# One evacuation step for two heads, with DMAs that bring the halves to the heads' tiles

## The chip, the cores and the metric

The kernel runs on one core of a Trainium2 chip. A core has a matrix engine (TensorE, PE in the profile, with its weight loads shown apart as PEld), three engines for elementwise work (VectorE, DVE; ScalarE, ACT; GpSimd, POOL) and a queue engine (SyncE, SP) that issues most of the DMAs here. Every engine works through its own instructions in order; semaphores make one wait for another. Matrix products land in PSUM, and ACT or DVE must bring them from there to SBUF ("evacuate" them) before TensorE can use them as operands or the PSUM tile can be filled again.

The metric is the device time of one execution in microseconds (us). Before the change it is 707.76 us, the median of three runs (707.51 to 709.02).

## The reference

One layer on a sequence of 1024 tokens of width 1024. The input is normalised and modulated to `u`; one projection `h = u @ w_in` gives queries, keys, values, gates and forget logits for 8 + 8 heads of width 64. Eight heads are forgetting attention, eight stick-breaking attention, both causal; the gated outputs go through `w_out`, a residual and a last layer norm.

```
h = u @ w_in
fq, fk, fv, fg, ff, sq, sk, sv, sg = _split_columns(h)
# forgetting heads
s = einsum('bhqd,bhkd->bhqk', q, k) * scale + (f_q[..., :, None] - f_k[..., None, :])
p = softmax(where(causal, s, -inf));  y = p @ v
# stick-breaking heads
z = einsum('bhqd,bhkd->bhqk', q, k) * scale
later = cumsum(log_keep, axis=3, reverse=True) - log_keep
w = where(strict, exp(log_sigmoid(z) + later), 0);  y = w @ v
y = concat([y_fox * silu(fg), y_sb * silu(sg)]) @ w_out
x = layer_norm(alpha * x + gate * y, ln_g, ln_b)
```

## The kernel before

**Precision.** All large products take fp32 values as a rounded part ("hi") and a rest ("lo"), and add three products: hi by hi, lo by hi, hi by lo. So each evacuation of queries and keys makes two pieces: a rounded copy on ACT and the rest (product minus the rounded copy) on DVE.

**Pairs.** The 16 heads are handled as eight pairs `p` = 0 to 7; 0 to 3 are stick-breaking, 4 to 7 forgetting. A pair's two heads `h` stand in the two halves of the 128 partitions of a projection: head 0 in partitions 0 to 63, head 1 in 64 to 127. Pairs 0 and 1 are projected in a start phase; the later ones by `gen_m(p, m)` with `m` = 0 for queries, 1 for keys and 2 for gates. `gen_m` fetches two weight halves (`fetch_m`), and then makes two chunks `ch` of 512 tokens, each 24 matmuls (L256 to L258) into one of two PSUM tiles `acc`, and evacuates each chunk at its end.

**The tiles of the heads.** For each head, `qst[p][h]` holds the rounded queries in the head's own 64 partitions and the rest in the other 64. `kst[p][h]` holds the rounded keys twice, once in each half. One matmul over all 128 partitions (L410) then gives hi by hi plus lo by hi. The third product (L411) takes the keys' rest, `klo[p]`, which holds both heads, against a query tile that is zero in the other head's partitions.

**The evacuation of queries and keys.** `evac_q` (L227) makes, for each head, one ACT step (L232) and one DVE step (L233) on 64 partitions. DVE writes its result into the other half of partitions. `evac_k` (L236) makes, for each head, one ACT step (L241), one DMA that copies the rounded keys to the other half (L243), and one DVE step (L244).

**The ring.** Split weights lie in a ring `whi`/`wlo` of five slots (`RING = 5`, `ring_w`). A weight half is fetched raw by SP into one of two raw tiles (L121), and split by POOL into a ring slot (L125, L126). A slot is free when the last matmul that reads it has run. Value weights, the output weights (which go back to DRAM, L770 and L771) and the attention outputs that are read back at the end (L788 to L792) use the same ring.

**Attention.** A unit is a pair, a head and a block of 128 queries; there are 128 units. A unit has scores (L410, L411), a softmax or stick-breaking part on ACT, DVE and POOL, a transpose on PE (L456) two units later, and the product with the values (L471).

**What sets the order.** The order of TensorE's instructions is written out by hand: the loop at L927 emits a unit's scores, and between them steps of the list `fillers` (projections, values) as the table `FILL` says. The last projection of keys, `gen_m(7, 1)`, ends just before the units of pair 7 begin. Pair 7 starts with the last block, which needs keys of all 1024 tokens. The orders of ACT, DVE, POOL and SP come from a planner at build time: it plays the program on a timeline of its own and gives each engine the earliest-written instruction that is ready there. On the chip each queue keeps that order, whatever is ready first. Around pair 7 SP also loads attention outputs (`yr`, L788), the residual input (`xr`, L823) and the output weights (`woh`, `wol`, L761 and L762). ACT's queue loads a forget row (`fb`, L375).

Of the kernel before, what the change touches and what calls it, by code (L numbers as in the profile page):

```python
# [8 lines left out]
F32 = mybir.dt.float32  # L9
F32R = mybir.dt.float32r  # L10
AF = mybir.ActivationFunctionType
ALU = mybir.AluOpType

P = 128
# [4 lines left out]
HD = 64  # L19
EPS = 1e-5  # L20
ALPHA = 2.0 ** 0.25
SCALE = HD ** -0.5
# [5 lines left out]
def tile_hybrid_layer(  # L28
# [17 lines left out]
    nc = tc.nc  # L46
# [15 lines left out]
    def acc_tile(name):  # L62
        return ps.tile([P, 512], F32, tag="acc", bufs=2, name=name)
# [52 lines left out]
    def ring_w(key):  # L116
        return [sb.tile([P, 528], F32R, tag=tag, bufs=RING, name=f"{tag}_{key}") for tag in ("whi", "wlo")]
# [14 lines left out]
    def fetch_m(p, m):  # L132
        return [fetch_half(p, m, h) for h in range(2)]
# [93 lines left out]
    def evac_q(p, ch, acc, qst, heads):  # L227
        s = slice(ch * 512, ch * 512 + 512)
        for h in heads:
            r = slice(h * HD, h * HD + HD)  # L230
            o = slice((1 - h) * HD, (1 - h) * HD + HD)
            nc.scalar.activation(qst[h][r, s], acc[r, :], AF.Copy, scale=SCALE)  # L232
            nc.vector.scalar_tensor_tensor(qst[h][o, s], acc[r, :], SCALE, qst[h].bitcast(F32)[r, s],  # L233
                                           op0=ALU.mult, op1=ALU.subtract)

    def evac_k(p, ch, acc, kst, klo, heads):  # L236
        s = slice(ch * 512, ch * 512 + 512)
        for h in heads:
            r = slice(h * HD, h * HD + HD)
            o = slice((1 - h) * HD, (1 - h) * HD + HD)  # L240
            first = nc.scalar.copy(kst[h][r, s], acc[r, :])  # L241
            kf = kst[h].bitcast(F32)
            nc.sync.dma_start(kf[o, s], kf[r, s])  # L243
            last = nc.vector.tensor_tensor(klo[r, s], acc[r, :], kf[r, s], op=ALU.subtract)  # L244
        return first, last

    def evac_g(p, ch, acc, sg):
        s = slice(ch * 512, ch * 512 + 512)
        nc.scalar.activation(sg[:, s], acc, AF.Tanh, scale=0.5)
        nc.vector.scalar_tensor_tensor(sg[:, s], sg[:, s], 1.0, acc, op0=ALU.add, op1=ALU.mult)  # L250

    def m_step(acc, tiles, kt, ch):
        hi, lo = tiles[kt // 4]
        c = slice((kt % 4) * P, (kt % 4) * P + P)
        s = slice(ch * 512, ch * 512 + 512)
        nc.tensor.matmul(acc, hi[:, c], u_hi[kt][:, s], start=(kt == 0), stop=False)  # L256
        nc.tensor.matmul(acc, hi[:, c], u_lo[kt][:, s], start=False, stop=False)  # L257
        nc.tensor.matmul(acc, lo[:, c], u_hi[kt][:, s], start=False, stop=(kt == NB - 1))  # L258

    qst, kst, klo, sgt, vt = {}, {}, {}, {}, {}  # L260
# [11 lines left out]
    def evac_m(p, m, ch, acc, heads=(0, 1)):  # L272
        if m == 0:
            evac_q(p, ch, acc, qst[p], heads)
        elif m == 1:
            return evac_k(p, ch, acc, kst[p], klo[p], heads)
        else:
            evac_g(p, ch, acc, sgt[p])

    def gen_m(p, m):  # L280
        tiles = fetch_m(p, m)
        yield
        (make_q, make_k, make_g)[m](p)
        for ch in ((1, 0) if m == 2 and p >= 4 else (0, 1)):
            acc = acc_tile(f"m_{p}_{m}_{ch}")
            for kt in range(NB):
                m_step(acc, tiles, kt, ch)
                if kt == NB - 1:
                    evac_m(p, m, ch, acc)
                if kt % 2 == 1:  # L290
                    yield

# [426 lines left out]
    for kb in range(NB):  # L719
# [5 lines left out]
        if kb < len(evacs):  # L725
            n, h = evacs[kb]
# [140 lines left out]
    def gen_last_g(p):  # L867
# [12 lines left out]

    fillers = chain([
        beside(chain([gen_v(0, v0_w, range(4, NB)), gen_m(1, 2)]), gen_gate()),
        gen_m(2, 0), gen_m(2, 1), gen_v(1),
        beside(chain([gen_m(2, 2), gen_m(3, 0), gen_m(3, 1), gen_m(3, 2)]), gen_forget()),
        gen_m(4, 0), gen_m(4, 1), gen_v(2),
        beside(chain([gen_m(4, 2), gen_m(5, 0), gen_m(5, 1), gen_m(5, 2),
# [40 lines left out]
    for k in range(len(units) + LAG + 1):  # L927
        if k < len(units):
# [10 lines left out]
            p, h, i = units[k]  # L939
# [85 lines left out]
```

## Time and profile before

| | |
|---|---|
| time, median of 3 runs | 707.76 us (707.51 to 709.02) |
| profiled execution, first to last instruction (span) | 705.8 us |
| PE busy | 680.8 us, 96% of the span |
| PE weight loads | 593.0 us, 84% |
| DVE busy | 509.6 us, 72% |
| POOL busy | 422.4 us, 60% |
| ACT busy | 378.8 us, 54% |
| DMA queue of SP | 32.4% of 16 engines' span |

Of the profiled execution the profile tells the span alone; the median of the runs is 1.96 us above it. Times in the profile are counted from the first instruction. A row of the timeline gives start, duration, engine, line, operation, what it writes and reads, shape, and in brackets the idle time of the engine before it and what ended that. A row of the groups gives count, busy time and the mean duration in ns, then the idle time before. A row of the waits gives who waited for whom, the total, the times and the longest. A busy PE is made of matmuls whose ends are modelled and which overlap, so its gaps are read from the waits.

### The profile page before, as it was taken

To read this page: it belongs to the slowest core of one execution; us is meant where nothing else is said; L and a number is where in the kernel's file an instruction comes from. 1 tells how busy PE (TensorE), PEld (TensorE's weight loads), DVE (VectorE), ACT (ScalarE), POOL (GpSimd) and SP (SyncE) were. 2 spreads that over 40 slices of the span, in tenths; PEclk is the share of its full clock that TensorE was granted. 3 is DMA by queue.
4 is the path that set the end of the run, shared out by engine and by line. 5 is a ranking of instruction groups with operands and counts; after the bars stand their busy time and mean duration, and the time that the engine had idled before them with its cause. 6 is when DMAs were issued, how large, how long until landed. Compare 5 with 4: busy or idle time off the path is not lost. (4 is left out here: it accounts for less than half of the span.)

```text
span 705.8 us, 11791 instructions
## 1 busy us (share of the span) xinstructions
PE 680.8 (96%) x4033; PEld 593.0 (84%) x4033; DVE 509.6 (72%) x963; ACT 378.8 (54%) x856; POOL 422.4 (60%) x523
## 2 busy tenths in 40 slices
PE   7999998989999999999999999999999999999995
PEld 4789887878998888889998887889988889888884
DVE  5985689897858697788686685757676767774644
ACT  4667346756658566666665563646564666621000
POOL 4560258665629675857388897868583455665412
PEclk9999999999999999999999999999999999999999
DMA  8953451101101212112034554435241189143301
GB/s 306 415 212 126 132 167 35 28 26 53 53 7 37 70 37 67 43 38 68 9 124 155 176 170 137 134 105 165 92 148 53 56 271 371 48 162 113 121 32 59
DMA packets 44027, 81.59 MB, mean 116 GB/s; under 512 B 5120, under 2 KB 18880, under 8 KB 43072
## 3 DMA queue, kind: packets, MB, share of 16 engines
q1 hardware_dynamic: 42816, 76.65, 32.4%
q10 hardware_dynamic: 1152, 4.19, 2.1%
q8 instruction: 32, 0.52, 0.3%
q14 instruction: 27, 0.22, 0.1%
HBM read 60.34 MB, written 16.29 MB: 109 GB/s over the span
## 5 line engine op out<-in xcount | busy, mean ns | idle before, releaser
L256 PE MATMUL m<-uh,whi 128*128 128x512 f32 x304 | 126.4, 416 | 0.0
L257 PE MATMUL m<-ul,whi 128*128 128x512 f32 x304 | 119.9, 394 | 0.0
L258 PE MATMUL m<-uh,wlo 128*128 128x512 f32 x304 | 119.7, 394 | 0.0
L459 DVE TENSOR_TENSOR pt<-T,pt 128x512 fp32r<-128x512 f32 (+2 forms) x192 | 100.5, 549 | 14.6 <-ACT pt L458 13.3
L439 POOL TENSOR_TENSOR be<-be,kp 128x127 f32<-128x127 f32 (+3 forms) x64 | 79.0, 1235 | 47.0 <-DVE kp L437 44.3
L458 ACT CAST pt<-T 128x512 fp32r<-128x512 f32 (+2 forms) x192 | 85.8, 480 | 18.6 <-PE T L456 14.8
L471 PEld LDWEIGHTS pv<-pt,v 128*128 128x128 f32 x640 | 83.9, 188 | 10.4 <-DVE pt L459 5.2
L471 PE MATMUL pv<-pt,v 128*128 128x256 f32 (+1 forms) x640 | 85.1, 277 | 4.5 <-DVE pt L459 3.6
L437 DVE TENSOR_TENSOR_SCAN kp<-kp 128x128 f32<-128x128 f32 (+6 forms) x56 | 82.6, 1476 | 1.9
L424 POOL TENSOR_SCALAR a<-a,l 128x1024 f32<-128x1024 f32 (+3 forms) x64 | 48.3, 755 | 41.7 <-DVE l L423 28.1
L422 ACT ACTIVATE a<-a,nm 128x1024 f32<-128x1024 f32 (+3 forms) x64 | 49.8, 779 | 40.8 <-DVE nm L417 38.9
L410 PE MATMUL S<-k,q 128*128 128x512 f32 (+5 forms) x192 | 66.8, 349 | 2.3 <-ACT be L430 1.7
L258 PEld LDWEIGHTS m<-uh,wlo 128*128 128x128 f32 x304 | 57.1, 188 | 13.6
L411 PE MATMUL S<-kl,qz 128*128 128x512 f32 (+5 forms) x192 | 65.5, 342 | 0.0
L256 PEld LDWEIGHTS m<-uh,whi 128*128 128x128 f32 x304 | 57.3, 189 | 8.8 <-DVE kl L244 0.4
L257 PEld LDWEIGHTS m<-ul,whi 128*128 128x128 f32 x304 | 57.4, 189 | 8.0
L480 POOL TENSOR_TENSOR ty<-ty,sg 64x256 f32<-64x256 f32 x64 | 48.8, 762 | 19.7 <-DVE ty L479 9.8
L434 DVE TENSOR_TENSOR_SCAN kp<-kp,ident 128x128 f32<-128x128 f32 x64 | 42.0, 656 | 24.4 <-ACT kp L429 21.1
L417 DVE CUSTOM_DVE_ANT_0 a<-S,fb 128x1024 f32<-128x1024 f32 (+3 forms) x64 | 48.2, 754 | 15.7 <-issue 6.5
L429 ACT ACTIVATE kp<-S 128x128 f32<-128x128 f32 (+3 forms) x64 | 41.7, 652 | 32.9 <-PE S L411 31.4
L126 POOL TENSOR_TENSOR wlo<-raw,whi 128x512 fp32r<-128x512 f32 x38 | 56.8, 1496 | 3.4 <-DMA wo_dr<-wlo_o 1.8
L311 PE MATMUL v<-whi_v,uh 128*128 128x256 f32 (+1 forms) x192 | 56.0, 292 | 1.1 <-DVE kl L244 1.1
(280 smaller groups left out, 1633.2 us busy)
## 6 DMA issues: line engine op xcount, KB each, us to landing
raw<-in_w_qkg_dram SPq DMA_DIRECT2D x38, 256.0 KB, 2.7
wss<-in_w_ss_dram SPq DMA_DIRECT2D x7, 1024.0 KB, 8.5
x<-in_x_dram SPq DMA_DIRECT2D x8, 512.0 KB, 7.6
k<-k SPq DMA_DIRECT2D x32, 128.0 KB, 2.2
wg<-in_w_gate_dram SPq DMA_DIRECT2D x8, 512.0 KB, 5.2
raw_o<-in_w_out_dram SPq DMA_DIRECT2D x16, 256.0 KB, 2.6
fb<-f_dr ACTq DMA_DIRECT2D x8, 512.0 KB, 4.2
wo_dr<-whi_o SPq DMA_DIRECT2D x16, 256.0 KB, 2.5
```

The costliest lines, as they stand in the source:

```text
L126: nc.gpsimd.tensor_tensor(lo[:, :n], raw, hi.bitcast(F32)[:, :n], op=ALU.subtract)
L256: nc.tensor.matmul(acc, hi[:, c], u_hi[kt][:, s], start=(kt == 0), stop=False)
L257: nc.tensor.matmul(acc, hi[:, c], u_lo[kt][:, s], start=False, stop=False)
L258: nc.tensor.matmul(acc, lo[:, c], u_hi[kt][:, s], start=False, stop=(kt == NB - 1))
L311: nc.tensor.matmul(acc[:, :n], u_hi[kt][:, ts_], hi[:, s], start=(kt == 0), stop=False)
L410: nc.tensor.matmul(S[:, s, :w], qst[p][h][:, qs], kst[p][h][:, ks], start=True, stop=False)
L411: nc.tensor.matmul(S[:, s, :w], z, klo[p][:, ks], start=False, stop=True)
L437: nc.vector.tensor_tensor_scan(rv, rv, rv, initial=kp[:, ke - P:ke - P + 1], op0=ALU.mult, op1=ALU.min)
L439: nc.gpsimd.tensor_tensor(be[:, :ke - 1], be[:, :ke - 1], kp[:, 1:ke], op=ALU.mult)
L458: nc.scalar.copy(hi[:, :n, qo:qo + P], t3)
L459: nc.vector.tensor_tensor(lo[:, :n, qo:qo + P], t3, hi.bitcast(F32)[:, :n, qo:qo + P], op=ALU.subtract)
L471: nc.tensor.matmul(acc[:, q0:256], vt[p][:, kb, h * P:(h + 1) * P], pt[:, kb % 4, q0:], start=(part == 0 and kb == 0), stop=(part == 1 and ...
```

## The change

For pairs 2 to 7 the chunks of queries and keys are evacuated by two new functions. Each makes one ACT step and one DVE step on all 128 partitions, that is on both heads at once. The pieces that belong to other partitions or to the other head's tile are brought there by DMAs on SP's queue.

For queries, the rounded part and the rest go to a pair of tiles from the ring `whi`/`wlo`, and four DMAs of 64 partitions carry them from there to `qst`. For keys, ACT writes both heads' rounded keys into `kst[p][0]`, and DVE makes `klo` in one step. Then two DMAs copy head 1's rows to both halves of `kst[p][1]`, and a third copies head 0's rows over head 1's rows in `kst[p][0]`. The start phase (pairs 0 and 1) keeps the old functions.

```diff
+    def evac_q_pair(p, ch, acc, qst):
+        s = slice(ch * 512, ch * 512 + 512)
+        hi, lo = (t[:, :512] for t in ring_w(f"q_{p}_{ch}"))
+        nc.scalar.activation(hi, acc, AF.Copy, scale=SCALE)
+        nc.vector.scalar_tensor_tensor(lo, acc, SCALE, hi.bitcast(F32), op0=ALU.mult, op1=ALU.subtract)
+        for part in range(2):
+            for h in range(2):
+                r = slice(h * HD, h * HD + HD)
+                to = slice((h ^ part) * HD, (h ^ part) * HD + HD)
+                nc.sync.dma_start(qst[h].bitcast(F32)[to, s], (hi, lo)[part].bitcast(F32)[r, :])
+
+    def evac_k_pair(p, ch, acc, kst, klo):
+        s = slice(ch * 512, ch * 512 + 512)
+        a, b = slice(0, HD), slice(HD, P)
+        nc.scalar.copy(kst[0][:, s], acc)
+        nc.vector.tensor_tensor(klo[:, s], acc, kst[0].bitcast(F32)[:, s], op=ALU.subtract)
+        k0, k1 = (t.bitcast(F32) for t in kst)
+        nc.sync.dma_start(k1[b, s], k0[b, s])
+        nc.sync.dma_start(k1[a, s], k0[b, s])
+        nc.sync.dma_start(k0[b, s], k0[a, s])
+
...
                 if kt == NB - 1:
-                    evac_m(p, m, ch, acc)
+                    if m == 0:
+                        evac_q_pair(p, ch, acc, qst[p])
+                    elif m == 1:
+                        evac_k_pair(p, ch, acc, kst[p], klo[p])
+                    else:
+                        evac_m(p, m, ch, acc)
```

## The prediction

> **What bounds the kernel now.** I read the page's sums first, then the busy time by stretches, then TensorE's waits in the stretch of the change.
>
> ```profile
> PE 680.8 (96%) x4033; PEld 593.0 (84%) x4033; DVE 509.6 (72%) x963; ACT 378.8 (54%) x856; POOL 422.4 (60%) x523
> ```
>
> ```profile
> 150.00:572.00 422.00, 417.38 (x2621) 373.13 (x2619) 307.90 (x597) 253.74 (x593) 285.30 (x335) 1.00 0.28 86
> 572.00:692.00 120.00, 119.77 (x611) 100.38 (x610) 77.55 (x164) 35.97 (x90) 58.40 (x75) 1.00 0.43 156
> ```
>
> The columns after the window's length are PE, PE weight loads, DVE, ACT, POOL, the granted clock, the DMA engines' busy share and GB/s. All changed evacuations lie between 150 and 572 us. There TensorE is busy 417.4 of 422 us at full clock, and after that, until its last matmuls, 119.8 of 120. Its order is fixed, so a stall there comes out at the end nearly whole, and a gain can't be larger than the waits it still has:
>
> ```profile
> PE pv L471 <- DVE pt L459: 2.1, 3, 1.5
> PE v L311 <- DVE kl L244: 1.1, 1, 1.1
> PE pv L471 <- ACT pt L458: 0.7, 1, 0.7
> PE S L410 <- DVE nm L417: 0.4, 1, 0.4
> ```
>
> These are all its waits from 150 to 572 us: 2.1 + 1.1 + 0.7 + 0.4 = 4.3 us. That is the most that the change can win. Only the second (1.1 us) is on an instruction that the change touches. So TensorE bounds this stage, not ScalarE (254 of 422 us) or VectorE (308).
>
> Here a rule speaks the other way. The Trainium skill, page "Perfetto Trace Analysis", section "Identifying the Most-Contended Engine", says that matmul busy time is a poor measure of TensorE's headroom and that the weight loads' share should be used. By it 422 − 373.1 = 48.9 us would be open here, and the 13.8 us of ScalarE time below could come off whole. The waits in the rows above contradict that: 4.3 us is what TensorE waited for others.
>
> **The change part by part.** *ACT and DVE steps.* By shape, the groups are:
>
> ```profile
> L233 DVE SCALAR_TENSOR_TENSOR q<-m,q 64x512 fp32r<-64x512 f32 x24 | 16.5, 688 | 6.6 <-ACT q L232 6.1
> L244 DVE TENSOR_TENSOR kl<-m,k 64x512 fp32r<-64x512 f32 x24 | 16.5, 686 | 4.8 <-ACT k L241 4.6
> L232 ACT ACTIVATE q<-m 64x512 fp32r<-64x512 f32 x24 | 14.2, 592 | 7.9 <-PE m L258 7.2 <-DVE q L233 0.2
> L241 ACT CAST k<-m 64x512 fp32r<-64x512 f32 x24 | 13.9, 581 | 10.9 <-PE m L258 8.8 <-DVE kl L244 1.9
> L250 DVE SCALAR_TENSOR_TENSOR sg<-sg,m 128x512 f32<-128x512 f32 x14 | 9.5, 679 | 2.2 <-ACT sg L249 2.2
> L249 ACT ACTIVATE sg<-m 128x512 f32<-128x512 f32 x14 | 8.4, 597 | 5.3 <-PE m L258 5.3
> ```
>
> The gate rows show that 128 partitions cost what 64 do (597 against 592 ns, 679 against 688 ns). So 48 ACT steps (14.2 + 13.9 = 28.1 us) become 24 of 597 ns (14.3 us): 13.8 us less. 48 DVE steps (33.0 us) become 24 of 679 ns (16.3 us): 16.7 us less. Neither engine sets the end, so this counts only through the waits above. The 1.1 us wait is this place:
>
> ```profile
> 184.74 0.69 DVE L244 TENSOR_TENSOR kl<-m,k 64x512 fp32r<-64x512 f32 x1
> 185.49 0.39 PE L311 MATMUL v<-whi_v,uh 128*128 128x264 f32 x1 [1.10 <-DVE kl L244]
> ```
>
> The second head's DVE step frees the PSUM tile late. With one step per chunk it goes: −1.1 us. What is late next there is nothing that the waits show. The other 3.2 us come from transposes and softmax, which the change doesn't touch; the engines' busy time falls by 5% (13.8 of 253.7 and 16.7 of 307.9), and as waits in a queue fall faster than the load I estimate −0.4 us (bounds 0 and −3.2). Relief: −1.5 us, bounds 0 and −4.3.
>
> *SP's queue.* Queries get 4 DMAs a chunk (48 in all), keys 3 where they had 2 (12 more): 60 more issues.
>
> ```profile
> L243 SPq DMA_DIRECT2D k<-k x32: 461/472/588, 49.8 to 569.3; - x32
> DMA to landing us min/median/max: 2.2/2.2/7.5
> ```
>
> 60 × 0.472 = 28.3 us of SP's time over 422 us, and 60 × 128 KB = 7.9 MB on DMA engines that are 28% busy. What they delay on SP's queue (raw weights, outputs of heads) has slack: no wait of TensorE above names a DMA. So 0. Without that cover it costs at most what a transfer lies behind, four issues or 1.9 us at each of 12 chunks. The queries themselves are needed many units later, and 2.2 us of landing lies beside projections.
>
> *The third copy of keys.* It overwrites rows that DVE and the first two copies read, so it waits on SP until these have landed, and everything behind it on SP waits too. Mostly nobody is near: the keys of pairs 2 to 6 are finished long before their scores. The last chunk of pair 7 is the exception:
>
> ```profile
> 565.85 0.58 ACT L241 CAST k<-m 64x512 fp32r<-64x512 f32 x1 [0.75 <-PE m L258]
> ```
>
> ```profile
> 566.46 0.47 SPq L243 DMA_DIRECT2D k<-k  x1
> 568.32 0.36 SPq L788 DMA_DIRECT2D yr<-y_dr  x1
> 568.77 0.44 SPq L823 DMA_DIRECT2D xr<-in_x_dram  x1
> 569.30 0.47 SPq L243 DMA_DIRECT2D k<-k  x1
> 569.82 0.61 SPq L762 DMA_DIRECT2D wol<-wo_dr  x1
> 570.48 0.54 SPq L761 DMA_DIRECT2D woh<-wo_dr  x1
> ```
>
> ```profile
> 571.76 0.40 PE L410 MATMUL S<-k,q 128*128 128x512 f32 x1
> ...
> 577.64 0.50 PE L410 MATMUL S<-k,q 128*128 128x512 f32 x1
> ```
>
> The matmul at 571.76 is the second half of pair 7's first scores (head 0). Before, its copy left at 566.46, with 5 us to spare. The matmul at 577.64 is head 1's; its copy left at 569.30. After, ACT ends at 566.4, the two head 1 copies leave at 566.5 and 566.9 (0.47 apart) and land 2.2 to 2.7 us later, at about 569.3. Only then can the third leave, and it now carries head 0's keys. That is the moment of the old copy at 569.30, whose landing, that of the one at 566.46, and that of `woh` (570.48) are:
>
> ```profile
> L243 SPq DMA_DIRECT2D k<-k x1: 467/467/467, 569.3 to 569.3; - x1
> DMA to landing us min/median/max: 7.5/7.5/7.5
> ...
> L243 SPq DMA_DIRECT2D k<-k x1: 467/467/467, 566.5 to 566.5; - x1
> DMA to landing us min/median/max: 2.7/2.7/2.7
> ...
> DMA to landing us min/median/max: 9.1/9.1/9.1
> ```
>
> Behind the two large loads (568.32 and 568.77) the copy took 7.5 us, to 576.8. So the matmul waits from 571.76 to 576.8: +5.0 us, and TensorE, in order, with it. The nearest bounds: 0, if it lands in the median 2.2 us (569.3 + 2.2 = 571.5); and +7.8, if it falls behind the output weights' first loads too and lands with `woh` (570.5 + 9.1 = 579.6). Below 0 nothing is possible, since the scores can't start earlier than TensorE's order has them. I take +5.0, the row at the same moment. Of it comes back what TensorE waits for others later, 0.2 us (the gap of 0.23 in 120 us, above): −0.2.
>
> On this place two rules of the Trainium skill's page "DMA: Bandwidth & Descriptors" pull apart. Its section "Anatomy of one DMA" gives a fixed 2.0 us plus bytes over 436 GB/s (fitted on another path), 2.3 us for 128 KB; the copy would then land in time and the sum be 5 us lower. Its section "Queues, rings and completion order" says that descriptors of a queue are consumed in ring order, which puts the copy behind the loads before it. The 7.5 us row agrees with the second.
>
> *The ring.* The 12 query chunks now also take a slot of the five. POOL fills every slot as soon as it is free:
>
> ```profile
> 157.87 0.63 POOL L125 TENSOR_SCALAR whi_v<-raw_v 128x528 fp32r<-128x528 f32 x1 [0.71 <-PE m L257]
> ...
> 396.61 0.40 PE L258 MATMUL m<-uh,wlo 128*128 128x512 f32 x1
> ...
> 401.10 0.40 PE L256 MATMUL m<-uh,whi 128*128 128x512 f32 x1
> ```
>
> The first row is a weight split that waited for a slot. So at the end of a query's first chunk there is often no free slot. Its evacuation then waits until the first weight half is freed, 12 matmuls later. From there to the first matmul of the next projection, which needs the same PSUM tile, I count 4.1 us in the tightest place (397.0 to 401.1, last two rows). The evacuation takes 0.60 + 0.68 us and its turn on two busy engines. I price that at +0.4 us in all; bounds 0, and six times the 1.1 us wait above, 6.6 us. A query tile holds its slot for 0.60 + 0.68 + 4 × 0.47 + 2.2 = 5.4 us, by which the next weights come later. That is hidden where they are split more than 5.4 us ahead of use, so 0.
>
> *Sum.* −1.5 + 5.0 − 0.2 + 0.4 = +3.7 us. The profiled span of 705.8 us becomes 709.5; the median stands 1.96 us above the span, so 711.5 us.
>
> **Rivals.** *(A) The copy lands in time.* The planner puts the third copy ahead of the two loads, or these come later. For it: the median copy lands in 2.2 us, and 571.5 is before 571.76. Against it: the loads are ready at 568.3 and 568.8, half a microsecond before the copies have landed. Then −1.5 + 0.4 gives 706.7 us, not slower, and with all waits gone 703.5, faster. It is decided by whether the landing is before 571.8 us on the old clock.
>
> *(B) The copy lands behind the output weights.* The distance from 569.3 to 569.82 is short, and the planner's clock is not the chip's. Then +7.8 in place of +5.0: 714.3 us.
>
> *(C) The ring binds.* Late query evacuations or late weights stall TensorE at each of the six query projections, +6.6 in place of +0.4, on top of the forecast: 717.7 us. For it: all five slots are in use. Against it: 4.1 us of room for 1.3 us of work.
>
> **How the numbers follow.** I count a change under 0.2% (1.4 us) as the same; about that is what a measurement of this kernel can tell. Chances: forecast 0.46 (its own range 709.3 to 713), A 0.27, B 0.14, C 0.13. The bound of 706.3 lies just below A's 706.7, and its relief is open downward to 703.5: I split A into faster 0.15 and same 0.12. All else is slower: 0.73. The range leaves out A's lowest part and C's highest: 705.5 to 716.5.
>
> **What would show it.** In the changed kernel's timeline, the third copy of pair 7's last chunk leaves after the loads `yr` and `xr` and lands some 7 us later; the second half of the first scores of pair 7 has a wait of about 5 us on a DMA of `k`, and this is TensorE's largest wait after 150 us. The wait of 1.1 us on `kl` is gone. There are 24 ACT and 24 DVE steps of 128x512 for queries and keys at about 0.6 and 0.7 us, and TensorE's other waits change by less than 2 us. The prediction is wrong if the copy lands before the scores, if TensorE waits on weights (`whi`, `wlo`) or on the PSUM tiles of `m`, or if its waits on `pt` grow because the planner's new order serves transposes later.

## The result and the profile after

The changed kernel takes 742.43 us (median) against 707.88 us for the kernel before on the same chip: 1.0477 times as long over all runs, 95% interval 1.0453 to 1.0502. By the medians it is 34.6 us slower. The forecast was 711.5 us, slower by 3.7, with an upper bound of 716.5. So the sign was right, and the size was wrong by 31 us.

The page of the kernel after, its busy time, and then its span and clock:

```profile
PE 694.1 (94%) x4033; PEld 601.7 (81%) x4033; DVE 496.2 (67%) x939; ACT 365.5 (49%) x832; POOL 419.0 (57%) x523
```

```profile
core 0: 740.8 us, clock 0.980
```

The span grew from 705.8 to 740.8 us, by 35.0. ACT and DVE each lost 13 us of busy time (378.8 to 365.5, 509.6 to 496.2). TensorE runs the same 4033 matmuls, yet is busy for 13.3 us longer (680.8 to 694.1). The mean granted clock fits this: 0.998 before and 0.980 after, so 0.002 of 705.8 us (1.4 us) were lost to it before and 0.020 of 740.8 us (14.8 us) after, 13.4 us more.

The rest are waits. These are TensorE's waits between 150 and 610 us of the kernel after (who waited for whom: total us, times, the longest):

```profile
PE m L281 <- POOL wlo L126: 10.6, 7, 3.1
PE S L438 <- DMA k<-k: 4.8, 1, 4.8
PE m L279 <- POOL whi L125: 4.1, 4, 2.0
PE v L339 <- POOL whi_v L125: 2.5, 1, 2.5
PE pv L499 <- DVE pt L487: 2.3, 3, 1.5
PE v L341 <- POOL wlo_v L126: 1.7, 2, 0.9
PE pv L499 <- ACT pt L486: 0.6, 1, 0.6
PE T L484 <- DVE pt L487: 0.4, 1, 0.4
```

Four of the eight rows are waits for split weights (tiles `whi`, `wlo`; those of the values have `_v`), of which the kernel before had none after 150 us: 10.6 + 4.1 + 2.5 + 1.7 = 18.9 us. The copy of keys adds 4.8. What is left, 2.3 + 0.6 + 0.4 = 3.3 us, is less than the 4.3 us of before, and the wait on `kl` is gone. Together: 18.9 + 4.8 − 1.0 + 13.3 = 36.0 us, for 35.0 measured. (Before 150 us TensorE's waits are 1.4 us fewer, 10.5 against 11.9 us, which brings the sum to 34.6.)

**Where the weights went.** The keys of pair 3 show it. Their first weight half was, in the kernel before, split by POOL and then first read by TensorE at these times (start, duration; POOL's timeline, then PE's):

```profile
224.87 0.61 POOL L125 TENSOR_SCALAR whi<-raw 128x512 fp32r<-128x512 f32 x1
...
227.40 2.67 POOL L126 TENSOR_TENSOR wlo<-raw,whi 128x512 fp32r<-128x512 f32 x2
```

```profile
254.80 0.39 PE L256 MATMUL m<-uh,whi 128*128 128x512 f32 x1
```

The second row joins two splits that end at 230.07, so the weights lay ready for 24.7 us. In the kernel after, the timeline of all engines reads so around the same matmul:

```profile
256.26 0.60 ACT L251 ACTIVATE whi_q<-m 128x512 fp32r<-128x512 f32 x1 [0.76 <-PE m L281]
...
256.90 0.69 DVE L252 SCALAR_TENSOR_TENSOR wlo_q<-m,whi_q 128x512 fp32r<-128x512 f32 x1 [0.47 <-ACT whi_q L251]
...
257.83 1.33 POOL L125 TENSOR_SCALAR whi<-raw 128x512 fp32r<-128x512 f32 x2
...
258.50 0.50 PE L279 MATMUL m<-uh,whi 128*128 128x512 f32 x1 [1.35 <-POOL whi L125]
258.83 0.40 PE L280 MATMUL m<-ul,whi 128*128 128x512 f32 x1
...
259.13 2.49 POOL L126 TENSOR_TENSOR wlo<-raw,whi 128x512 fp32r<-128x512 f32 x2
260.44 0.50 PE L281 MATMUL m<-uh,wlo 128*128 128x512 f32 x1 [1.21 <-POOL wlo L126]
```

POOL splits the keys' weights only after the second query chunk has been evacuated (256.26 to 257.59), at the moment when TensorE wants them. The first of the two `wlo` splits joined in the row of 259.13 ends at 260.38. The raw weights were there long before. This is the tile `raw` of the kernel after, for loads issued between 217 and 222 us:

```profile
L121 SPq DMA_DIRECT2D raw<-in_w_qkg_dram x2: 334/334/334, 217.9 to 220.6; - x2
...
DMA to landing us min/median/max: 2.5/2.6/2.6
```

The later load landed by 220.6 + 2.6 = 223.2 us, over 34 us ahead of its split. Counted in both kernels from the end of the `wlo` split to the first matmul of the keys, the lead went from 24.7 us to −1.9 us (258.50 − 260.38): that matmul, which needs `whi` alone, starts before the split of `wlo` has ended. At all six passages from queries to keys the lead is now between −1.8 and −3.8 us.

**The keys of pair 7.** SP's timeline of the kernel after, the matmul that waits, and the third copy's landing (tile `k`):

```profile
595.58 0.47 SPq L266 DMA_DIRECT2D k<-k  x1
596.09 0.60 SPq L267 DMA_DIRECT2D k<-k  x1
...
597.78 0.37 SPq L816 DMA_DIRECT2D yr<-y_dr  x1
598.25 0.43 SPq L851 DMA_DIRECT2D xr<-in_x_dram  x1
598.78 0.47 SPq L268 DMA_DIRECT2D k<-k  x1
```

```profile
605.59 0.54 PE L438 MATMUL S<-k,q 128*128 128x512 f32 x1 [4.81 <-DMA k<-k]
```

```profile
L268 SPq DMA_DIRECT2D k<-k x1: 468/468/468, 598.8 to 598.8; - x1
DMA to landing us min/median/max: 6.7/6.7/6.7
```

This is the forecast's case, later by what was lost before it: the third copy leaves right behind `yr` and `xr`, lands 6.7 us after its issue, and the second half of pair 7's first scores waits 4.8 us.

**The clock.** Windows of the kernel after (window, length, busy time of PE, PEld, DVE, ACT, POOL, then the granted clock, the DMA share and GB/s):

```profile
320.00:324.00 4.00, 3.76 (x13) 3.27 (x14) 0.42 (x1) 0.61 (x2) 3.35 (x5) 0.50 0.42 131
...
328.00:332.00 4.00, 4.00 (x22) 3.37 (x21) 3.45 (x4) 2.74 (x6) 3.46 (x4) 1.00 0.40 108
```

TensorE is busy nearly throughout the first, but at a clock of 0.50: 13 matmuls fit into 4 us, where the row at full clock, 328 to 332 us, has 22. Counted over the clock record of the trace, the clock is 0.5 at six places between 261 and 609 us (from 261.1, 319.1, 418.1, 496.6, 575.1 and 605.9; 6.8 us at the second, 3.4 us at each other), each beside waits; together 23.8 us. TensorE still waits in 1.2 us of them, and half of the rest, 11.3 us, is lost. The kernel before has no such place between 150 and 690 us.

### The profile page after: what moved, and what is told of

It is laid out like the page before. It is cut to its first block, busy times and chain, and to the rows that moved or that the text cites. A ratio compares the mean times of both kernels' runs of the same rounds, so it can differ in the third digit from the quotient of the medians.

```text
span 740.8 us, 11870 instructions
## 1 busy us (share of the span) xinstructions
PE 694.1 (94%) x4033; PEld 601.7 (81%) x4033; DVE 496.2 (67%) x939; ACT 365.5 (49%) x832; POOL 419.0 (57%) x523
## 4 chain that ended last, share of the span: by engine, by line
PE 62%; issue 5%; POOL 5%; DMA 5%; DVE 4%; ACT 2%; SPq 1%; POOLq 0%; ACTq 0%; DVEq 0%
PE pv L499 8%; PE m L281 7%; PE T L484 7%; PE m L279 7%; PE m L280 7%; PE o L839 4%; PE o L841 4%; PE o L840 4%; PE S L439 3%; PE S L438 3%; PE v L341 3%; PE v L339 3%; PE v L340 3%; DMA raw<-in_w_qkg_dram 2%; POOL wlo L126 1%
## 5 line engine op out<-in xcount | busy, mean ns | idle before, releaser
L279 PE MATMUL m<-uh,whi 128*128 128x512 f32 x304 | 128.8, 424 | 4.2 <-POOL whi L125 4.1
L281 PE MATMUL m<-uh,wlo 128*128 128x512 f32 x304 | 122.6, 403 | 10.6 <-POOL wlo L126 10.6
L280 PE MATMUL m<-ul,whi 128*128 128x512 f32 x304 | 121.6, 400 | 0.0
L486 ACT CAST pt<-T 128x512 fp32r<-128x512 f32 (+2 forms) x192 | 86.0, 481 | 24.7 <-PE T L484 20.7
L499 PEld LDWEIGHTS pv<-pt,v 128*128 128x128 f32 x640 | 86.6, 195 | 10.2 <-DVE pt L487 4.8
L499 PE MATMUL pv<-pt,v 128*128 128x256 f32 (+1 forms) x640 | 86.9, 282 | 4.7 <-DVE pt L487 4.0
L416 ACT CAST qz<-q 64x128 fp32r<-64x128 f32 x128 | 37.4, 295 | 46.3 <-PE S L439 40.8
```

Source lines behind the costliest of these rows:

```text
L486: nc.scalar.copy(hi[:, :n, qo:qo + P], t3)
L499: nc.tensor.matmul(acc[:, q0:256], vt[p][:, kb, h * P:(h + 1) * P], pt[:, kb % 4, q0:], start=(part == 0 and kb == 0), stop=(part == 1 and ...
```

## The experiments

**Theories.** The theory after the result: two separate causes. First, the order in which ring slots are handed out. By the theory a slot's turn comes in the order in which the program asks, and the keys' weights are asked for behind the two query tiles; so the planner can place their split only when the second query chunk has been evacuated, and the lead of the weights is gone. Second, the third copy of keys, as forecast. The slower clock adds to both. The rivals for the larger part: the ring's capacity (five slots are too few for weights and query tiles together, in whatever order), and the load of 48 more DMAs on SP and the DMA engines, which would delay raw weights. Times below are medians, and differences are each to the kernel before on the same chip (706.5 to 707.5 us).

**Keys alone, queries alone.** Each kernel makes one half of the change:

```diff
 k_only
-                    if m == 0:
-                        evac_q_pair(p, ch, acc, qst[p])
-                    elif m == 1:
+                    if m == 1:
                         evac_k_pair(p, ch, acc, kst[p], klo[p])
                     else:
                         evac_m(p, m, ch, acc)
 q_only
                     if m == 0:
                         evac_q_pair(p, ch, acc, qst[p])
-                    elif m == 1:
-                        evac_k_pair(p, ch, acc, kst[p], klo[p])
                     else:
                         evac_m(p, m, ch, acc)
```

> Keys in one step for both heads, queries by the old functions. Theory (order of the ring): the query tiles in the ring cause all but the late third key copy, so this is the kernel before plus the copy's wait of about 5 us, less about 1 us of relief: 711 to 713 us, with one wait of some 5 us on a DMA of k at the start of pair 7 and no waits on whi or wlo. Rival (load on the queues): 12 of the 60 added DMAs are here, so besides the copy's 5 us about a fifth of the other 29 us stays: 717 to 720 us.

> Queries in one step for both heads through the ring, keys by the old functions. Theory (order of the ring): the six waits on key weights stay, the wait on the key copy goes: 735 to 738 us. Rival (the key copies hold up the queue, and so the weights): the waits on whi and wlo shrink by half or more: below 725 us.

Keys alone: 712.28 us, +5.8 (ratio 1.0077, 1.0052 to 1.0102). Queries alone: 737.90 us, +31.4 (1.0431, 1.0389 to 1.0474). Both came out as the theory expected. So nine tenths of the loss are the queries'. (The two halves add up to 37.2 us, not 34.6: in `q_only`, where the keys are evacuated by the old function, TensorE's wait on `kl` grows from 1.1 to 2.9 us.) TensorE's largest wait with keys alone, and the two windows in which the clock is at half speed. TensorE waits until 574.90 us:

```profile
PE S L436 <- DMA k<-k: 4.4, 1, 4.4
```

```profile
573.31:576.72 3.41, 1.82 (x7) 1.66 (x7) 0.59 (x1) 0.30 (x1) 0.00 (x0) 0.50 1.04 364
576.72:580.14 3.42, 3.42 (x14) 2.94 (x13) 1.96 (x6) 1.87 (x4) 0.81 (x2) 0.51 0.92 349
```

One wait of 4.4 us brings 6.8 us at half clock. In 1.6 us of them TensorE still waits; in the other 5.2 us (1.82 + 3.42) it works at half speed, which costs 2.6 us. The whole is 7.0 us; the other waits of that profile are 1.6 us fewer than before, and 5.4 us is near the 5.8 measured.

**The keys' weights asked for first.** All of the change stays; only the place where the keys' weights are asked for moves ahead of the query tiles:

```diff
 key_weights_first
+    ahead = {}
     def gen_m(p, m):
-        tiles = fetch_m(p, m)
+        tiles = ahead.pop((p, m), None) or fetch_m(p, m)
+        if m == 0:
+            ahead[p, 1] = fetch_m(p, 1)
```

> The changed kernel, but the fetch of the key weights is written ahead of the query projection, so that the ring gives them their slots before the query tiles; the ring, the DMAs and the steps are the same. Theory (order): the waits on whi and wlo after each query projection go, and what stays is the key copy at pair 7: 711 to 715 us. Rival (capacity): five slots are too few with the two query tiles in them, so something else in the ring comes late and the time stays above 730 us. Rival (load of the 60 added DMAs): unchanged, 738 to 745 us.

It takes 714.80 us, +8.3 (1.0120, 1.009 to 1.015) where the change has +34.6: 26.3 us are gone, with the same five slots, the same query tiles in them and the same DMAs. TensorE's waits from 150 to 620 us:

```profile
PE S L442 <- DMA k<-k: 4.6, 1, 4.6
PE pv L503 <- DVE pt L491: 3.1, 3, 1.3
PE S L442 <- DVE nm L449: 1.5, 2, 1.1
PE pv L503 <- ACT pt L490: 0.7, 1, 0.7
```

No row names a weight, as the theory expected (711 to 715 us). That settles the place: there are as many slots and as many DMAs as in the change, and only the order of asking differs. Neither the ring's capacity nor the load is the main cause. The order of asking also moves the loads of raw weights ahead of the query copies on SP's queue, so this run does not tell a late slot from a late load; `slot_only` and `slot_held` below bear on that.

**Which head's keys come last.** ACT writes the rounded keys into head 1's tile in place of head 0's, so that the chain of copies ends with keys of head 1, whose scores come later:

```diff
 mirror
-        nc.scalar.copy(kst[0][:, s], acc)
-        nc.vector.tensor_tensor(klo[:, s], acc, kst[0].bitcast(F32)[:, s], op=ALU.subtract)
+        nc.scalar.copy(kst[1][:, s], acc)
+        nc.vector.tensor_tensor(klo[:, s], acc, kst[1].bitcast(F32)[:, s], op=ALU.subtract)
-        nc.sync.dma_start(k1[b, s], k0[b, s])
-        nc.sync.dma_start(k1[a, s], k0[b, s])
-        nc.sync.dma_start(k0[b, s], k0[a, s])
+        nc.sync.dma_start(k0[a, s], k1[a, s])
+        nc.sync.dma_start(k0[b, s], k1[a, s])
+        nc.sync.dma_start(k1[a, s], k1[b, s])
```

> The changed kernel, with the roles of the key tiles exchanged: both heads' keys are written to head 1's tile, the first two copies fill head 0's tile, and the third serves head 1, whose scores in pair 7 come 6 us later. Theory: the wait of 4.8 us on the key copy goes, with its share of slower clock, and nothing else changes: 736 to 738 us. Rival (the first scores of pair 7 would then wait for something else that is as late, such as the forget row): within 2 us of the changed kernel, 740 to 743 us.

It takes 737.06 us, +30.6 (1.0417, 1.0376 to 1.0457), 4.0 us less than the change and as expected. No wait on a copy of keys is left among TensorE's waits; those on the weights of projections stay as they were (10.5 and 4.3 us on `wlo` and `whi`). The expectation that nothing else changes did not hold: the waits on value weights fall from 4.2 to 0.3 us, and those of `pv` on DVE's `pt` grow from 2.3 to 5.2 us. The second cause is the third copy, and it is separate from the first.

**A ring slot without a DMA.** Is it the turn in the ring alone, or the time for which the DMAs hold a slot? This kernel is the kernel before, in which each of the 12 query chunks also takes a slot and writes one column to it; the queries go the old way, so the extra writes are work that the result does not use:

```diff
 slot_only (on the kernel before)
                 if kt == NB - 1:
+                    if m == 0:
+                        hi, lo = ring_w(f"idle_{p}_{ch}")
+                        nc.scalar.copy(hi[:, :1], acc[:, :1])
+                        nc.vector.tensor_copy(lo[:, :1], acc[:, :1])
                     evac_m(p, m, ch, acc)
```

> The kernel before with its old evacuations and not one DMA more; at the end of each query chunk of pairs 2 to 7 a pair of ring tiles is taken, one column is written to each, and nothing reads them. Theory (order of the ring): the turn alone costs, since the key weights, written later, get no slot before the second query chunk ends: 728 to 738 us, with waits on whi and wlo like those of the changed kernel. Rival (capacity: what costs is that the query tiles hold their slots while four DMAs empty them): here they hold them for under 1 us, so 706 to 710 us.

It takes 724.31 us, +17.6 (1.0252, 1.0231 to 1.0272): less than the 728 to 738 us expected, and far more than the rival's 706 to 710. TensorE waits for the keys' weights at the same places in pairs 2, 3, 4 and 7, and not in pairs 5 and 6 (waits of this kernel from 150 to 620 us):

```profile
PE m L258 <- POOL wlo L126: 5.7, 4, 2.3
...
PE m L256 <- POOL whi L125: 2.8, 4, 1.3
```

A slot that is written for one column and read by no DMA is enough for more than half of the loss. Waits on weights are 9.6 us of it (with 1.1 on value weights). The mean clock of 0.992 over 722.2 us loses 4.4 us more than before, and the waits on `pt` and `kl` grow by 3.4 us, to which the 24 small steps on ACT and DVE may add. But 31.4 − 17.6 = 13.8 us of the queries' loss need something more.

**A slot held by DMAs.** The same with 64 columns, and four DMAs that read them from the slot into an unused place in DRAM, so that the slot stays taken for nearly as long as in the change (from the start of the evacuation to the issue of the last DMA 2.4 us on average, with whole query tiles in `q_only` 2.7 us):

```diff
 slot_held (on the kernel before)
+                    if m == 0:
+                        hi, lo = ring_w(f"idle_{p}_{ch}")
+                        nc.scalar.copy(hi[:, :64], acc[:, :64])
+                        nc.vector.tensor_copy(lo[:, :64], acc[:, :64])
+                        for part in range(2):
+                            for h in range(2):
+                                r = slice(h * HD, h * HD + HD)
+                                nc.sync.dma_start(held[part, r, :], (hi, lo)[part].bitcast(F32)[r, :64])
                     evac_m(p, m, ch, acc)
```

> The kernel of the turn alone, where in addition four small DMAs on the sync queue read each pair of ring tiles, so that the tiles hold their slots some 4 us, as the query tiles do; the evacuations are the old ones (64 columns are written instead of one). The turn alone cost 17.6 us, the query change with its ring tiles 31. Theory (the rest of 13 us is the hold, which delays the next weights where the output weights use the ring as well): 732 to 738 us, with waits on weights between 400 and 510 us, which the turn alone had not. Rival (the rest comes from the steps for both heads or from the large DMAs): 723 to 727 us.

It takes 730.56 us, +23.1 (1.0363, 1.0308 to 1.0419; its four runs spread from 729.4 to 737.4): between the two forecasts. The stage from 400 to 520 us, in which the output weights also pass through the ring, shows what the hold with its DMAs adds. Waits of TensorE there, in `slot_only`, in `slot_held` and with the whole query half of the change (`q_only`):

```profile
PE v L317 <- POOL wlo_v L126: 1.1, 2, 0.9
```

```profile
PE m L259 <- POOL wlo L127: 2.2, 2, 1.9
PE v L322 <- POOL wlo_v L127: 1.0, 1, 1.0
```

```profile
PE m L281 <- POOL wlo L126: 5.0, 2, 3.7
PE v L339 <- POOL wlo_v L126: 1.1, 2, 0.8
PE v L337 <- POOL whi_v L125: 0.6, 1, 0.6
```

On weights 1.1, 3.2 and 6.7 us. The time for which the slot is held hardly explains the last step (2.4 and 2.7 us to the last issue, and 1.8 and 2.3 us of landing behind it). The largest wait, at the keys of pair 5, comes by another way. POOL's timeline of `q_only` there:

```profile
420.98 0.62 POOL L125 TENSOR_SCALAR whi<-raw 128x512 fp32r<-128x512 f32 x1 [4.10 <-DMA raw<-in_w_qkg_dram]
421.56 2.51 POOL L126 TENSOR_TENSOR wlo<-raw,whi 128x512 fp32r<-128x512 f32 x2
```

POOL's order puts the `whi` split of the second weight half ahead of the `wlo` splits, and that half's raw weights are late. In each of the three kernels their load leaves SP behind two DMAs of output weights. In `slot_only` it leaves at 407.6 us and lands after 2.8 us; in `slot_held`, with the four small DMAs ahead too, it leaves at 411.9 and lands after 5.3; in `q_only`, with the four query copies ahead, at 413.8 and lands after 7.0. TensorE's wait on `wlo` at this place is 0, 1.9 and 3.7 us. The whole change shows the same (the load leaves at 409.5 us, POOL waits 2.53 us for it, TensorE 2.17 us on `wlo`). So in this stage the load on SP's queue, which `key_weights_first` excluded as the main cause, has a part.

Hold and small DMAs together are worth 23.1 − 17.6 = 5.5 us, to be taken with the spread above. Of the other 31.4 − 23.1 = 8.3 us, the profiles (735.5 and 727.7 us) show 3.5 us in waits, those at pair 5 among them, and 3.8 us in clock (0.982 against 0.987). No run separated the 512 columns from the planner's other order. With the weights asked for first 3.7 us are left of the queries' 31.4 (`q_first`, below).

**Both mended.** The keys' weights first, and the copies in the mirrored order:

> Both mends together: key weights written ahead of the query projection, and the key tiles' roles exchanged. Theory: both of the changed kernel's costs go, and the relief of ScalarE and VectorE is left: 0 to 2 us under the kernel before, 704.5 to 707 us. Rival (the steps for both heads cost something of their own, in DMA load or in turns on the queues): 708 to 711 us.

It takes 708.74 us, +2.1 (1.0026, 1.0014 to 1.0037). So two edits, which leave the number and shape of the evacuation steps as they are, take away 32.5 of the 34.6 us. But the gain that the change could bring does not appear: 704.5 to 707 us were expected, and the time fell to the rival (708 to 711 us, steps that cost something of their own). TensorE's waits from 150 to 620 us:

```profile
PE pv L503 <- DVE pt L491: 3.1, 3, 1.3
PE S L442 <- DVE nm L449: 2.7, 3, 1.6
PE pv L503 <- ACT pt L490: 0.7, 1, 0.7
```

The 1.1 us on `kl` are gone, and `pt` (2.1 before) and `nm` (0.6 before, in this stretch) have grown by 1.0 + 2.1 = 3.1 us. That is 2.0 us more of waits, for 2.1 us more of time.

**Parts of it, without pair 7's keys.** `k_mirror` is the key half with mirrored copies; `k_but_last` the key half for pairs 2 to 6 only; `first_but_last` the keys' weights first, with the new keys for pairs 2 to 6 only; `q_first` the query half alone, with the keys' weights first.

```diff
 k_but_last
-                    if m == 0:
-                        evac_q_pair(p, ch, acc, qst[p])
-                    elif m == 1:
+                    if m == 1 and p < NPAIR - 1:
                         evac_k_pair(p, ch, acc, kst[p], klo[p])
 first_but_last (with the edit of key_weights_first)
-                    elif m == 1:
+                    elif m == 1 and p < NPAIR - 1:
                         evac_k_pair(p, ch, acc, kst[p], klo[p])
```

> Keys alone in one step for both heads, with the key tiles' roles exchanged; queries by the old functions, the ring as before. Theory: 1 to 2 us under the kernel before (the wait of TensorE on the keys' rest at 185 us goes, and no copy is late): 704.5 to 706 us. Rival (the third copy, now head 1's, is late for its scores 6 us later): a wait on a DMA of k at the second unit of pair 7, and 708 us or more.

> Keys of pairs 2 to 6 in one step for both heads; the keys of pair 7, whose scores follow at once, and all queries by the old functions; the ring as before. Theory: no late copy, the wait of 1.1 us at the values of pair 2 gone, nothing added: 704 to 706.5 us, at or under the kernel before. Rival (the third copy's wait on the queue costs something in the other pairs too): over 707.5 us.

> The changed kernel with the key weights written ahead of the query projection, and with the keys of pair 7 by the old function. Theory: both costs gone and a relief of 1 us or so: 705 to 707.5 us. Rival (what was left over the kernel before with both mends, 2 us, comes from the query steps and their 48 DMAs): 708 to 709 us, and well over the kernel with keys alone.

> Queries in one step for both heads, key weights written ahead of the query projection, all keys by the old functions. Theory (the order of the ring was nearly all of the query change's cost): 706 to 709 us, with no waits on whi or wlo. Rival (the query tiles' hold on the slots costs by itself): over 712 us, with waits on weights of later projections.

| kernel | us | ratio to before | 95% |
|---|---|---|---|
| k_mirror | 708.41 | 1.0022 | 1.0002 to 1.0041 |
| k_but_last | 706.14 | 0.9995 | 0.998 to 1.001 |
| first_but_last | 708.04 | 1.0025 | 1.0011 to 1.004 |
| q_first | 710.33 | 1.0057 | 1.004 to 1.0075 |

Keys without pair 7, at 706.14 us within the 704 to 706.5 expected, cost nothing and win nothing that can be measured, although the waits of that profile after 150 us are 1.3 us fewer than before. `first_but_last`, which adds the queries to these keys, takes 708.04 us, 1.9 us more and as its rival said: what both mends leave over comes with the query half. `k_mirror` missed its 704.5 to 706 us. The time is that of its rival, but not the place: the wait of 1.9 us on a copy of keys that is left stands at the first unit of pair 7, not the second, on the second copy, which landed 6.4 us after its issue. Its runs spread from 705.1 to 713.7 us. The query half costs 3.7 us even with the weights first, which missed the expectation of 706 to 709 us. No wait on weights is left in it; its profile, of an execution of 709.29 us, has 1.5 us more waits after 150 us than the kernel before, with one of 1.8 us on `kl` among them. What the slower executions lose beyond that has no row and stays open. No kernel here beats the kernel before.

## Why the prediction was right or wrong

**What bounds the kernel: right.** TensorE's 4.3 us of waits were taken as the ceiling for any gain, and no run contradicts it. ACT lost 13.3 us and DVE 13.4 us of busy time, and with both mends the kernel is not faster. The rule weighed there (the Trainium skill, page "Perfetto Trace Analysis", section "Identifying the Most-Contended Engine") would have left 48.9 us open for such relief; no run here shows any of it.

**ACT and DVE steps: right in size per step, the relief too high.** The groups of the kernel after by shape (count; busy us, mean ns; idle before):

```profile
L252 DVE SCALAR_TENSOR_TENSOR wlo_q<-m,whi_q 128x512 fp32r<-128x512 f32 x12 | 8.3, 689 | 6.4 <-ACT whi_q L251 3.9 <-DMA wo_dr<-wlo_o 2.4
L264 DVE TENSOR_TENSOR kl<-m,k 128x512 fp32r<-128x512 f32 x12 | 8.2, 684 | 2.7 <-ACT k L263 2.7
L251 ACT ACTIVATE whi_q<-m 128x512 fp32r<-128x512 f32 x12 | 7.2, 598 | 7.4 <-PE m L281 7.2
L263 ACT CAST k<-m 128x512 fp32r<-128x512 f32 x12 | 7.0, 586 | 9.0 <-PE m L281 9.0
```

598 and 586 ns stand against the 597 forecast, 689 and 684 against 679. The wait of 1.1 us on `kl` went. DVE's busy time fell by 13.4 us where the steps alone give 16.5, so its other steps took 3.1 us more. The estimate of −0.4 us on other waits held with keys alone (2.9 us beside the copy, where the kernel before has 3.4 beside `kl`), and failed with both halves: 6.5 us with both mends. That it is the planner's other order on DVE that delays `pt` and `nm` there is argued, not tested.

**SP's queue at nothing: right only where the weights have their lead.** With 60 more DMAs and the order mended, no wait on weights is left. Without the lead it is not nothing: at pair 5 a raw load behind the query copies kept POOL waiting 2.53 us and TensorE 2.17 us. The first row of the fence above shows one side effect that the step left out: 2.4 us in which DVE's query step waited for a DMA of output weights to leave the ring slot.

**The third copy: right in place, mechanism and size.** It was priced at +5.0 and the matmul waited 4.81 us. Between the two rules of the page "DMA: Bandwidth & Descriptors" of the Trainium skill the runs side again with the one in "Queues, rings and completion order": the copy behind two loads took 6.7 us, not the 2.3 that the other gives as an estimate. What came back after it was put at −0.2. In fact the half clock took more: 3.4 us at half speed behind that wait, 1.7 us lost, and 2.6 us lost in `k_only`.

**The ring: this is the step that failed.** It rested on two sentences. "POOL fills every slot as soon as it is free": not so for weights that are asked for behind another tile. And the query tile's hold of 5.4 us, "by which the next weights come later", was called hidden, by the lead of weights as the kernel before had it. But the delay is not 5.4 us from an unchanged start. In pairs 2, 3, 4 and 7 the split starts only 0.05 to 1.6 us after the evacuation of the second query chunk does, as if it had to wait until both query tiles have been given out. (That the order of asking decides is shown by `key_weights_first`; that the planner's handing out is what holds the split is argued from the code and from these times.) In pairs 5 and 6 the first split starts 1.2 and 2.8 us before that evacuation, and the late raw load of the second half holds up the rest. The lead of 24.7 us, which was to hide the delay, is itself what the change takes away. The +0.4 (bounds 0 and 6.6) for late evacuations looked at the wrong waiter: ACT began the query evacuations 0.03 to 0.9 us after their chunk's last matmul, and it was the weights behind them that came late. In its place the runs show 26.3 us, waits and clock together, the part that `key_weights_first` takes away. The row quoted for "no free slot" could have led there: it told that the ring is full, and the next question, in which order its slots are given, was not asked.

**Rival C** had the place (the ring, at each of the six query projections) and the wrong mechanism (capacity), and its 717.7 us was 25 us too low. (The range's upper bound of 716.5 lies below that figure, so the range left out rival C as a whole and not only its highest part.) The argument against it, 4.1 us of room for 1.3 us of work, concerned PSUM tiles and not slots.

**What was missing from the sum: the clock.** Every term was priced as the wait alone. The waits grew by 22.7 us (18.9 + 4.8 − 1.0), and TensorE's busy time by 13.3 us on top. Where a wait falls on the clock's windows (last section) is a matter of luck, so this term can be bounded ahead of a run but hardly told exactly.

## What to carry to other kernels

A temporary tile put into a ring that also holds prefetched data stops the prefetch of everything that the program asks for behind it, if slots are given out in the order of asking. Look for the first load that is asked for after the tile, compare its lead before with the time at which the tile becomes due, and move the asking for the load ahead (here 26.3 us of 34.6).

In a kernel bound by TensorE, price a new wait of TensorE with the clock beside it: here 22.7 us of waits brought 13.3 us more of slow matmuls, about 1.7 us for each window of 3.4 us at half clock. And where copies form a chain, let the chain end with the data that are needed last.

## What the runs showed of the hardware

A short wait in a busy stream can cost clock. Around 258 us the kernel after had two waits of 1.35 and 1.21 us with two matmuls between them (rows above), and the clock was 0.5 for 3.4 us from 261.1 on. But `q_only` has the same two waits, of 1.34 and 1.22 us, at 264.97 and 266.93 us, and no slow clock behind them. The windows of both (columns as above), first the kernel after, then `q_only`:

```profile
257.70:261.12 3.42, 1.41 (x5) 0.89 (x6) 2.76 (x2) 1.68 (x3) 3.42 (x5) 1.00 0.64 147
261.12:264.53 3.41, 3.41 (x13) 2.81 (x12) 3.38 (x3) 0.86 (x2) 1.49 (x3) 0.50 0.62 180
```

```profile
264.64:268.05 3.41, 1.86 (x7) 1.20 (x8) 3.21 (x2) 1.23 (x3) 3.41 (x4) 1.00 0.72 163
268.05:271.46 3.41, 3.41 (x21) 2.92 (x20) 3.41 (x4) 1.60 (x5) 1.48 (x3) 1.00 0.50 154
```

The windows are cut on a fixed grid. In each trace with several slow stretches they begin whole multiples of 3.413 us apart (in the kernel after 17, 46, 69, 92 and 101 of them behind the first, at 261.1 us), wherever the waits lie. TensorE was idle for 2.0 us of the first window (3.42 − 1.41), and the next ran at half clock; in `q_only` the same waits fell partly into the window before, 1.55 us of idle time were left (3.41 − 1.86), and the clock stayed. Counted over all thirteen traces between 140 and 690 us, every one of the 21 windows at full clock with more than 1.7 us of idle time is followed by one at half clock; between 1.6 and 1.7 us it is 3 of 13, and below 1.6 us one (1.47 us) of some two thousand. So the bound lies near half a window. In the two stretches of 6.8 us shown here TensorE went on waiting in the first slow window: 1.1 us from 319.1 us on in the kernel after, 1.6 us in `k_only`.

The Trainium skill, page "TensorE: Matmul & The Clock Gate", section "HAM oscillation — how this bites in real kernels", gives as its rule that there should be no gaps in TensorE's work above about 3.4 us. The length of the slow stretches agrees with the window of about 3.4 us that the same page of the Trainium skill gives in its section "What's actually happening". The rule does not hold here as a bound: idle time of 1.7 us within one window was enough, also when it was made of two shorter gaps.
